# Down projection of a two-layer mixer and gated-FFN network, as seven quadrant products of Strassen's form for eight

## The chip, the core and the metric

The kernel runs on one core of one Trainium2 chip. The metric is the device time of one execution in microseconds. The kernel before took a median of 1257.42 us over 3 runs (1256.32 to 1257.91).

## The reference

One sequence of 512 tokens with 1024 channels goes through two layers. A layer is a mixer (dilated attention, a retention and a gated linear attention beside it, then `w_out`), a residual with layer norm, a gated feed-forward network with a causal convolution of width 3, and again a residual with layer norm. Only the second half matters here:

```python
def conv_glu_ffn(x, w_up, conv_w, conv_b, w_down):
    u = causal_dwconv(x @ w_up, conv_w, conv_b)
    gate, val = jnp.split(u, 2, axis=-1)
    return (jax.nn.silu(gate) * val) @ w_down
...
        ffn = conv_glu_ffn(x, w_up[l], conv_w[l], conv_b[l], w_down[l])
        x = layer_norm(DEEPNORM_ALPHA * x + ffn, ln2_g[l], ln2_b[l])
```

All arrays are float32. `w_up` is 1024 x 5632 and `w_down` is 2816 x 1024, so the gated activations have 2816 = 22 x 128 channels.

## The kernel before

**Precision.** Every large product is made of three matmuls. Each operand is split into a high part, rounded to the matmul format float32r, and a low part that holds the rest; `mm3` (L202 to L205) adds high x high, high x low and low x high in the same accumulator. The high part is a copy on ScalarE, the low part a subtraction on VectorE.

**Weights.** The host packs all weights in order of use. `weight_tile` (L180) loads one tile of up to 128 x 1024 by a DMA that SP issues into `raw` (2 buffers), casts it on ScalarE to `whi` (L189) and subtracts on VectorE to `wlo` (L190); `whi` and `wlo` have 5 buffers each. `chunk` does so for all tiles of a product.

**Up projection.** The tokens lie in columns: `xth` and `xtl` hold the high and low part of the layer's input, 128 channels by 8 blocks by 512 tokens. For each of 22 blocks of 128 activation channels, `up` (L749) makes the gate and the value rows, 2 x 8 x 3 matmuls of 512 tokens. `conv` (L738) applies the convolution, one ScalarE pass (L741) and two VectorE ones (L742, L743). `glu` (L759) applies silu, multiplies (L762) and splits the activation in a high and a low page (L766, L767). A page is a 128 x 512 tile; pools named `pg`, `yt`, `yrg` and `rope` hold 9, 14, 8 and 4 of them.

**Down projection.** It is done in two halves of 11 activation blocks, f = 0 and f = 1, each behind its own part of the up projection. `token_gemm` (L383) makes, for each half h of the 1024 output columns, four accumulators of 128 tokens by 512 columns, with the activation page as the stationary operand and the weights as the moving one. `residual` (L377) adds an accumulator to the residual rows `x0` to `x3` on VectorE (L379), and for f = 1 collects statistics (L381). In the last call, f = 1 and h = 1, the last 9 k-steps go tile by tile, so that tile t is finished 27 matmuls ahead of tile t + 1:

```python
        for t in range(NT):
            for i in range(n - tail, n):
                step(i, t)
                if t >= 2 and i == n - tail + 3:
                    to_columns()
            done(ps[t], t)
```

`done` then normalises the tile with `norm_rows` (L343): a few small VectorE instructions for the scale, and four of 512 columns (L354, L357). In layer 1 the rows go out by DMA; in layer 0 `to_columns` (L364) transposes them on TensorE and splits them into the next `xth` and `xtl`.

**Order and buffers.** A scheduler orders each engine's instructions ahead of time by its own estimate of when each is ready; every engine then takes its list strictly in order. PSUM has 8 banks: 3 `acc`, 1 `side`, 4 `sm` (named bk). The pool `x4` has 3 buffers of 128 x 2048; during the feed-forward network one holds the norm's scale and shift (`gb`), which GpSimd's queue loads.

Of the kernel before, what the change touches and what calls it, by code (L numbers as in the profile page):

```python
# [17 lines left out]
P = 128  # L18
# [22 lines left out]
def weight_chunks():  # L41

    w = {}
    every = tuple(range(KD))
    c = (("w_in", 1536, 1792), ("w_in", 3072, 3088))
    w["ret_qk"] = [(ks, c) for ks in ((0, 1, 2), (3, 4, 5), (6, 7))]
    w["gla_q"] = [(every, (("w_in", 2304, 2432),))]
    w["gla_k"] = [(every, (("w_in", 2432, 2560),))]
    for name, c in (
        ("values", (("w_in", 1792, 2048), ("w_in", 2560, 2816))),  # L50
        ("heads0", heads(0)),
        ("v", (("w_in", 1024, 1536),)),
        ("heads1", heads(1)),
        ("gates", (("w_in", 2048, 2304), ("w_in", 2816, 3072))),
    ):
        w[name] = [(ks, c) for ks in PAIRS]
    for h in range(2):
        c = (("w_out", h * 512, h * 512 + 512),)
        w[f"out{h}"] = [(ks, c) for ks in (PAIRS[2], PAIRS[3], PAIRS[0], PAIRS[1])]
    for f in range(2):  # L60
        for j in range(NFH):
            m = (f * NFH + j) * P
            c = (("w_up", m, m + P), ("w_up", D_FF + m, D_FF + m + P))
            w[f"up{f}_{j}"] = [((0, 1, 2, 3), c), ((4, 5, 6, 7), c)]
        for h in range(2):
            c = (("w_down", h * 512, h * 512 + 512),)
            k0 = f * NFH
            w[f"down{f}_{h}"] = [(tuple(range(k0 + a, min(k0 + a + 2, k0 + NFH))), c) for a in range(0, NFH, 2)]
    return w

def width(cols):
# [69 lines left out]
def hymba(ctx: ExitStack, tc: tile.TileContext, x, xt, wpk, prm, wal, lnv, cst, out):  # L141
# [57 lines left out]
    def at(priority):  # L199
        tc.cur_priority = priority  # L200

    def mm3(ps, ah, al, bh, bl, first, last):  # L202
        nc.tensor.matmul(ps, ah, bh, start=first, stop=False)  # L203
        nc.tensor.matmul(ps, ah, bl, start=False, stop=False)  # L204
        nc.tensor.matmul(ps, al, bh, start=False, stop=last)  # L205

    mmul = nc.tensor.matmul
    V = nc.vector
# [196 lines left out]
    for l in range(DEPTH):  # L405
# [338 lines left out]
            return u  # L744

        stats = [sp.tile([P, 12], F32, tag="stats", name=nm("st"), bufs=8) for _ in range(NT)]
        for f in range(2):
            rows = []
            def up(pss, kt, cols, first, last, columns_at=()):  # L749
                for gv in range(2):  # L750
                    ms = slice(gv * P, (gv + 1) * P)
                    for k in range(KD):
                        h_, l_ = kt[k]
                        if gv * KD + k in columns_at:
                            to_columns()
                        mm3(pss[gv][:, cols], h_[:, ms], l_[:, ms], xth[:, k, cols], xtl[:, k, cols],
                            first and k == 0, last and k == KD - 1)

            def glu(pss, j):  # L759
                us = [conv(pss[gv], gv * NF + f * NFH + j) for gv in range(2)]  # L760
                A.activation(out=us[0], in_=us[0], func=AF.Silu)
                V.tensor_mul(us[1], us[0], us[1])  # L762
                tag = "yrg" if j < 4 else "yt"
                h_ = page(tag, 512, F32R)
                l_ = page(tag, 512, F32R)
                A.copy(h_, us[1])  # L766
                V.tensor_sub(l_, us[1], h_.bitcast(F32))  # L767
                rows.append((h_, l_))

            j0 = 0  # L770
            if f == 0:
                early_cols, late_cols = slice(0, S // 2), slice(S // 2, S)
                kts = [chunk(l, f"up{f}_{j}") for j in range(2)]
                pss = [[acc(), acc()], [acc(), side()]]
                up(pss[0], kts[0], early_cols, True, False)
                up(pss[1], kts[1], early_cols, True, False, (2, 15))
                for j in range(2):
                    up(pss[j], kts[j], late_cols, False, True)
                    glu(pss[j], j)
                j0 = 2  # L780
            for j in range(j0, NFH):
                kt = chunk(l, f"up{f}_{j}")
                pss = [acc(), acc()]
                up(pss, kt, slice(0, S), True, True)
                glu(pss, j)
            if f == 1:
                gb = load_gb(2 * l + 1)
                if l < DEPTH - 1:
                    xth = xp.tile([P, KD, S], F32R, tag="xth", name=nm("xth"))
                    xtl = xp.tile([P, KD, S], F32R, tag="xtl", name=nm("xtl"))  # L790
            for h in range(2):
                kt = chunk(l, f"down{f}_{h}")

                def done(ps, t):
                    residual(ps, t, h, ALPHA if f == 0 else 1.0, f == 1)
                    if f == 1 and h == 1:
                        norm_rows(t, gb, l == DEPTH - 1)
                        if l < DEPTH - 1:
                            pending.append(t)

                token_gemm(rows.__getitem__, kt, 9 if f and h else 4, done)

# [36 lines left out]
```

## Time and profile before

| what | value |
|---|---|
| median of 3 runs | 1257.42 us |
| the profiled execution, its own time | 1255.33 us |
| its span on the core | 1253.6 us |
| TensorE busy (PE) | 1233.8 us, 98% |
| VectorE busy (DVE) | 786.7 us, 63% |
| ScalarE busy (ACT) | 453.1 us, 36% |
| GpSimd busy (POOL) | 15.9 us, 1% |
| mean granted TensorE clock | 0.998 |
| read from HBM | 112.93 MB, 92 GB/s over the span |

Busy is the sum of the recorded durations, as a share of the span. Matmuls are pipelined and their ends are modelled, so that a busy TensorE can hold overlapping records. A group line of the profile has the line and engine, the operation, out<-in by the program's names, the shapes and the count, then busy us, mean ns of one, and the idle time before them with what ended it. A timeline line has start and duration in us; what stands in brackets is the idle time before it. A row of stretches has the stretch, its length, then for each engine busy us and (instructions), the granted clock, the DMA share and GB/s. A line of waits has the total, the count and the longest.

### The profile page before, as it was taken

Reading aid. Unit: us, or ns where it says so; the run is one execution under the profiler, and the core shown is the slowest. Engines: PE = TensorE matmul, PEld = TensorE weight load, DVE = VectorE, ACT = ScalarE, POOL = GpSimd, SP = SyncE. Lnnn points to the kernel's source line nnn. Section 1 sums busy time; section 2 is a strip of 40 time slices with the busy share of each in tenths; the row PEclk is TensorE's granted clock in tenths of the full one; section 3 lists DMA queues with packets and bytes.
Section 4 is the critical chain, followed back from the end, with each engine's and each line's share of the span. In section 5 each row is a group of like instructions: output and inputs, shape, how many; then the busy total and the mean of one; then the engine's idle time right before and its main releaser. Section 6 shows DMA issues by size and latency. Waiting matters only on the chain.

```text
span 1253.6 us, 15361 instructions
## 1 busy us (share of the span) xinstructions
PE 1233.8 (98%) x6020; PEld 1004.1 (80%) x6020; DVE 786.7 (63%) x1519; ACT 453.1 (36%) x629; POOL 15.9 (1%) x26
## 2 busy tenths in 40 slices
PE   9999999999999999999999999999999999999997
PEld 7777777798888888888887777778988888888885
DVE  5677676687664356664767757767766633566646
ACT  4413445135442134442142134451444422444410
POOL 0010000000000000000000000000000000000000
PEclk9999999999999999999999999999999999999999
DMA  8402322224233332232142023232333322333221
GB/s 289 135 18 68 101 68 74 95 67 126 93 89 105 93 101 92 93 101 76 61 134 85 1 68 101 68 102 67 96 107 101 101 76 93 118 101 102 93 76 67
DMA packets 33399, 116.01 MB, mean 93 GB/s; under 512 B 3728, under 2 KB 4144, under 8 KB 33200
## 3 DMA queue, kind: packets, MB, share of 16 engines
q1 hardware_dynamic: 32176, 110.85, 28.0%
q0 software_dynamic: 1152, 4.19, 1.0%
q8 instruction: 47, 0.77, 0.3%
q14 instruction: 24, 0.20, 0.0%
HBM read 112.93 MB, written 2.10 MB: 92 GB/s over the span
## 4 chain that ended last, share of the span: by engine, by line
PE 90%; DMA 4%; DVE 3%; ACT 2%; issue 0%; SPq 0%; DVEq 0%; ACTq 0%
PE acc L205 25%; PE acc L203 25%; PE acc L204 25%; DMA raw<-in_wpk 4%; PE bk L277 3%; PE side L204 2%; PE side L203 2%; PE side L205 2%; DVE wlo L190 2%; ACT whi L189 2%; PE bk L636 2%; PE bk L606 1%; PE side L277 1%; PE bk L529 1%; PE bk L535 1%; PE bk L549 1%
## 5 line engine op out<-in xcount | busy, mean ns | idle before, releaser
L190 DVE TENSOR_TENSOR wlo<-raw,whi 128x1024 fp32r<-128x1024 f32 (+2 forms) x201 | 240.2, 1196 | 227.3 <-ACT whi L189 226.2
L189 ACT CAST whi<-raw 128x1024 fp32r<-128x1024 f32 (+2 forms) x201 | 206.2, 1026 | 342.6 <-PE side L205 133.8
L204 PE MATMUL acc<-xtl,whi 128*128 128x512 f32 (+1 forms) x768 | 288.7, 376 | 0.0
L205 PE MATMUL acc<-xth,wlo 128*128 128x512 f32 (+1 forms) x768 | 288.6, 376 | 0.0
L203 PE MATMUL acc<-xth,whi 128*128 128x512 f32 (+1 forms) x768 | 288.6, 377 | 0.0
L203 PEld LDWEIGHTS acc<-xth,whi 128*128 128x128 f32 x768 | 144.2, 188 | 27.5 <-issue 1.5
L204 PEld LDWEIGHTS acc<-xtl,whi 128*128 128x128 f32 x768 | 144.5, 188 | 26.5 <-DVE xtl L375 0.4
L205 PEld LDWEIGHTS acc<-xth,wlo 128*128 128x128 f32 x768 | 144.5, 188 | 26.3
L205 PE MATMUL acc<-whi,xtl 128*128 128x512 f32 (+1 forms) x384 | 147.8, 385 | 0.0
L203 PE MATMUL acc<-whi,xth 128*128 128x512 f32 (+1 forms) x384 | 147.2, 384 | 0.6 <-ACT whi L189 0.6
L204 PE MATMUL acc<-wlo,xth 128*128 128x512 f32 (+1 forms) x384 | 145.8, 380 | 0.7 <-DVE wlo L190 0.7
L203 PE MATMUL acc<-whi,yt 128*128 128x512 f32 x238 | 93.1, 391 | 0.0
L205 PE MATMUL acc<-whi,yt 128*128 128x512 f32 x238 | 92.9, 390 | 0.0
L204 PE MATMUL acc<-wlo,yt 128*128 128x512 f32 x238 | 92.6, 389 | 0.0
L205 PEld LDWEIGHTS acc<-whi,xtl 128*128 128x128 f32 x384 | 72.1, 188 | 15.6 <-issue 3.9
L203 PEld LDWEIGHTS acc<-whi,xth 128*128 128x128 f32 x384 | 72.3, 189 | 15.1 <-issue 3.2
L204 PEld LDWEIGHTS acc<-wlo,xth 128*128 128x128 f32 x384 | 72.2, 188 | 15.1 <-issue 2.2
L742 DVE SCALAR_TENSOR_TENSOR pg<-acc,prm,pg 128x511 f32<-128x511 f32 x86 | 64.2, 747 | 31.8 <-ACT pg L741 31.8
L741 ACT ACTIVATE pg<-acc,prm 128x512 f32<-128x512 f32 x86 | 66.9, 778 | 26.4 <-PE acc L205 26.4
L743 DVE SCALAR_TENSOR_TENSOR pg<-acc,prm,pg 128x510 f32<-128x510 f32 x86 | 64.4, 749 | 3.0
L379 DVE SCALAR_TENSOR_TENSOR x<-x,acc 128x512 f32<-128x512 f32 x38 | 26.1, 687 | 61.8 <-PE acc L205 61.8
L203 PE MATMUL acc<-whi,yrg 128*128 128x512 f32 x138 | 54.4, 394 | 0.0
(176 smaller groups left out, 1523.9 us busy)
## 6 DMA issues: line engine op xcount, KB each, us to landing
raw<-in_wpk SPq DMA_DIRECT2D x188, 512.0 KB, 3.6
gb<-in_lnv POOLq DMA_DIRECT2D x8, 512.0 KB, 4.6
x<-in_x SPq DMA_DIRECT2D x4, 512.0 KB, 5.9
raw<-in_wpk SPq DMA_DIRECT2D x8, 256.0 KB, 2.8
out<-x SPq DMA_DIRECT2D x8, 256.0 KB, 2.0
raw<-in_wpk SPq DMA_DIRECT2D x4, 408.0 KB, 3.5
xraw<-in_xt SPq DMA_DIRECT2D x3, 512.0 KB, 7.5
cst<-in_cst SPq DMA_DIRECT2D x1, 1222.0 KB, 8.6
```

The source lines that it names most:

```text
L189: nc.scalar.copy(hi, raw)
L190: lo_engine.tensor_sub(lo, raw, hi.bitcast(F32))
L203: nc.tensor.matmul(ps, ah, bh, start=first, stop=False)
L204: nc.tensor.matmul(ps, ah, bl, start=False, stop=False)
L205: nc.tensor.matmul(ps, al, bh, start=False, stop=last)
L277: nc.tensor.transpose(dst, src, ident)
L379: V.scalar_tensor_tensor(out=xr, in0=xr, scalar=scale, in1=ps, op0=ALU.mult, op1=ALU.add)
L529: mmul(sc, kT, qbd, start=True, stop=True)
L636: mmul(oT[hh * 64:hh * 64 + 64, j * P:], vv[:, j, c0 + hh * 64:c0 + hh * 64 + 64], pts[hh][:, o:o + n], start=j == 0, stop=js == groups[-1])
L741: A.activation(out=u, in_=ps, func=AF.Identity, scale=w(2), bias=w(3))
L742: V.scalar_tensor_tensor(out=u[:, 1:], in0=ps[:, :S - 1], scalar=w(1), in1=u[:, 1:], op0=ALU.mult, op1=ALU.add)
L743: V.scalar_tensor_tensor(out=u[:, 2:], in0=ps[:, :S - 2], scalar=w(0), in1=u[:, 2:], op0=ALU.mult, op1=ALU.add)
```

## The change

The activations H (22 blocks by 512 tokens) and `w_down` are cut in quadrants. With the tokens 256 to 511 as "late" and 0 to 255 as "early", A11 and A21 are the late and early half of blocks 0 to 10, A12 and A22 those of blocks 11 to 21. B11 and B12 are the left and right 512 columns of the first 11 blocks of `w_down`, B21 and B22 those of the others. The eight quadrant products become seven, each of 11 k-steps by 2 token tiles of 128 by 3 matmuls:

- P11 = A11 B11 and P12 = A12 B21, added into the same two banks, alpha. Their 22 steps are put between the up projection's blocks 11 to 21, two a block. Between the two, ScalarE copies P11 out (`p1`, which takes one of the 5 `wlo` buffers).
- Four products in one pass over k: beta = S2 (B22 + B12 + B11), eps = A22 (B22 + B21 + B12 + B11), delta = R1 (B12 + B11), gamma = S3 (B22 + B12). They use all 8 banks. R1 = A22 - A21 and S3 = A11 - A21 replace A21 and A11 in place, on GpSimd, during the last blocks of the up projection; S2 = S3 + A22 is made on VectorE.
- zeta = (S2 - A12) B22, the last product; its operand replaces A12, on GpSimd.

In the pass each k-step loads its four weight quadrants as one tile of 128 x 2048 (1 MB) into `x4`, of which `gb` leaves two buffers. GpSimd makes four sums in place (L870 to L873), ScalarE casts the whole tile (L875) and VectorE makes its low part (L876), into halves of a tile that takes the place of `xth` and `xtl`. The activations are no longer split in `glu`, but per use: H[k] as it is (h0, l0) and the pair S2, A22 (h1, l1). Those of P11, P12 and zeta are split into `rope` pages (L798, L799).

After the pass VectorE combines: the early rows x0 and x1 need beta, eps, delta and gamma and are normalised while zeta runs; the late rows x2 and x3 need alpha, beta, delta and zeta.

```diff
-        for f in range(2):
-            rows = []
...
-            for h in range(2):
-                kt = chunk(l, f"down{f}_{h}")
...
-                token_gemm(rows.__getitem__, kt, 9 if f and h else 4, done)
+            if j >= NFH:
+                for _ in range(2 if j < NF - 2 else 1):
+                    st, k = steps.pop(0)
+                    st(k)
+                    if st is p11 and k == NFH - 1:
+                        p1 = wp.tile([P, 1024], F32, tag="wlo", name=nm("p1"), bufs=5)
+                        for i in range(2):
+                            A.copy(p1[:, i * 512:(i + 1) * 512], alpha[i])
...
+        while steps:
+            st, k = steps.pop(0)
+            st(k)
...
+        wth = xp.tile([P, 2, 4, 512], F32R, tag="xth", name=nm("wth"))
+        wtl = xp.tile([P, 2, 4, 512], F32R, tag="xtl", name=nm("wtl"))
+        beta, eps, delta, gamma = [bank(), bank()], [acc(), acc()], [acc(), side()], [bank(), bank()]
+        for k in range(NFH):
+            o, nk, w = offsets[l, f"dall{k}"][0]
+            raw = x4("wraw")
+            nc.sync.dma_start(out=raw.rearrange("p a c -> p (a c)"),
+                              in_=wpk[o:o + P * nk * w].rearrange("(p n) -> p n", p=P))
+            G.tensor_add(raw[:, 0, :], raw[:, 0, :], raw[:, 2, :])
+            G.tensor_add(raw[:, 2, :], raw[:, 2, :], raw[:, 3, :])
+            G.tensor_add(raw[:, 3, :], raw[:, 0, :], raw[:, 3, :])
+            G.tensor_add(raw[:, 1, :], raw[:, 3, :], raw[:, 1, :])
+            th, tl = wth[:, k % 2], wtl[:, k % 2]
+            A.copy(th, raw)
+            V.tensor_sub(tl, raw, th.bitcast(F32))
+            s2 = page()
+            V.tensor_add(s2[:, :256], S3(k), A22(k))
+            h0, l0 = two_parts(H[k], "pg")
+            h1, l1 = page("pg", 512, F32R), page("pg", 512, F32R)
+            for cs, src in ((slice(0, 256), s2[:, :256]), (slice(256, 512), A22(k))):
+                A.copy(h1[:, cs], src)
+                V.tensor_sub(l1[:, cs], src, h1[:, cs].bitcast(F32))
+            G.tensor_sub(A12(k), s2[:, :256], A12(k))
+            for ps, (ah, al), q, n in ((beta, (h1, l1), 0, 3), (eps, (h1, l1), 256, 1),
+                                       (delta, (h0, l0), 0, 2), (gamma, (h0, l0), 256, 0)):
+                for i in range(2):
+                    ts = slice(q + i * P, q + (i + 1) * P)
+                    mm3(ps[i], ah[:, ts], al[:, ts], th[:, n, :], tl[:, n, :], k == 0, k == NFH - 1)
...
+        p3 = product(zeta, "d22", A12)
+        for k in range(4):
+            p3(k)
+        for i in range(2):
+            early_rows(i)
...
+        for k in range(4, NFH - 3):
+            p3(k)
+        got = [p3(k, (0,)) for k in range(NFH - 3, NFH)]
...
+        late_rows(0)
+        to_columns()
+        for k, g in zip(range(NFH - 3, NFH), got):
+            p3(k, (1,), g)
+        to_columns()
+        late_rows(1)
```

How the order of instructions changes is shown at two places of layer 0. The first is the steady part of the down projection. In before, VectorE there splits weights for h = 1 (`wlo`) and takes up accumulators (`x_82` to `x_85` are the residual rows x0 to x3, `st` their statistics):

```order
L190 TENSOR_TENSOR wlo_4721<-raw_4718,whi_4720 128x1024
L379 SCALAR_TENSOR_TENSOR x_82<-x_82,acc_4568 128x512
L381 BN_STATS st_2375<-x_82 128x6
L379 SCALAR_TENSOR_TENSOR x_83<-x_83,acc_4569 128x512
L381 BN_STATS st_2376<-x_83 128x6
```

In the change VectorE's list in the pass repeats five instructions a step. Here is one step and the next step's low part (`wraw` is the raw weight tile, `wtl` its low part, `pg` are h1, l1, h0, l0 and s2, `yt` are activations):

```order
L773 TENSOR_TENSOR pg_4796<-yt_3158,pg_4795 128x512
L883 TENSOR_TENSOR pg_4800<-pg_4793,pg_4799 128x256
L883 TENSOR_TENSOR pg_4800<-yt_4176,pg_4799 128x256
L878 TENSOR_TENSOR pg_4838<-yt_3231,yt_4275 128x256
L876 TENSOR_TENSOR wtl_4416<-wraw_4785,wth_4415 128x2048
```

Each of these reads two tiles, and none of them an accumulator (`acc`, `bk` or `side`), where L379 reads one tile and one accumulator. GpSimd's list in before has nothing at this place but the load of `gb`, and goes on with the next layer:

```order
L717 DMA gb_4527<-in_lnv 128x1024 x2
L557 TENSOR_TENSOR pg_5441<-pg_5034,cst 128x128
L533 TENSOR_TENSOR pg_5447<-yrg_5206,cst 128x512
L557 TENSOR_TENSOR pg_5489<-pg_5034,cst 128x128
L533 TENSOR_TENSOR pg_5496<-yrg_5206,cst 128x512
```

In the change its list at the same steps is this:

```order
L870 TENSOR_TENSOR wraw_4785<-wraw_4785 128x512
L871 TENSOR_TENSOR wraw_4785<-wraw_4785 128x512
L872 TENSOR_TENSOR wraw_4785<-wraw_4785 128x512
L873 TENSOR_TENSOR wraw_4785<-wraw_4785 128x512
L884 TENSOR_TENSOR yt_4275<-pg_4838,yt_4275 128x256
```

So four sums of 512 columns and one difference of 256 stand on GpSimd for every step of the pass, and VectorE's low part of a tile (L876) follows its sums by way of ScalarE's cast.

The second place is the end of the layer. In before, TensorE ends with the last matmuls of tile x3 (`side`) and has the transposes of x1 (`cst` is the identity) in their midst:

```order
L205 MATMUL side_4751<-whi_4726,yt_4144 128x512
L277 MATMUL bk_4940<-cst,x_83 128x128 x4
L277 MATMUL bk_4947<-cst,x_83 128x128 x4
L203 MATMUL side_4751<-whi_4732,yt_4219 128x512
L204 MATMUL side_4751<-wlo_4733,yt_4219 128x512
```

In the change TensorE is at the fifth step, k = 4, of the last product (bk_4924 and bk_4925 are zeta; rope_5034 and rope_5035 the high and low rows of k = 4 and 5; x_82 is x0):

```order
L209 MATMUL bk_4925<-whi_4954,rope_4959 128x512
L207 MATMUL bk_4924<-whi_5030,rope_5034 128x512
L208 MATMUL bk_4924<-wlo_5031,rope_5034 128x512
L207 MATMUL bk_4925<-whi_5030,rope_5034 128x512
L208 MATMUL bk_4925<-wlo_5031,rope_5034 128x512
L281 MATMUL bk_5126<-cst,x_82 128x128 x4
L281 MATMUL bk_5133<-cst,x_82 128x128 x4
L209 MATMUL bk_4924<-whi_5030,rope_5035 128x512
```

VectorE reaches the last instructions of x0 (L361) and the low rows rope_5035 (L799) here:

```order
L907 BN_STATS st_2376<-x_83 128x6
L361 SCALAR_TENSOR_TENSOR x_82<-x_82,s_ln_4987,gb_4376 128x512 x2
L350 BN_AGGR s_ln_5009<-st_2376 128x2
L918 TENSOR_TENSOR x_85<-x_85,p_3882 128x512
L352 TENSOR_SCALAR s_ln_5011<-s_ln_5009 128x1
L358 SCALAR_TENSOR_TENSOR x_83<-x_83,s_ln_5009,gb_4376 128x512
L308 TENSOR_SCALAR s_ln_5013<-s_ln_5011 128x1
L358 SCALAR_TENSOR_TENSOR x_83<-x_83,s_ln_5009,gb_4376 128x512
L310 TENSOR_TENSOR s_ln_5014<-s_ln_5013 128x1
L799 TENSOR_TENSOR rope_5035<-yt_3767,rope_5034 128x256
```

From the first use of beta (L895) to rope_5035 VectorE's list has 26 instructions of 512 columns. Four steps of the last product and four matmuls of the fifth stand before the transposes of x0 on TensorE, and behind those the next matmuls wait for the rows of k = 4.

More of the change, by code (lines that the diff above doesn't have):

```diff
@@ L746, in hymba @@
         stats = [sp.tile([P, 12], F32, tag="stats", name=nm("st"), bufs=8) for _ in range(NT)]
-        for f in range(2):
-            rows = []
[L749 to L790, printed above, removed]
-            for h in range(2):
-                kt = chunk(l, f"down{f}_{h}")
[L794 to L799, printed above, removed]
-                token_gemm(rows.__getitem__, kt, 9 if f and h else 4, done)
@@ new lines, in hymba, with up, glu @@
+        H = []
+        def up(pss, kt, cols, first, last, columns_at=()):
+            for gv in range(2):
+                ms = slice(gv * P, (gv + 1) * P)
+                for k in range(KD):
+                    h_, l_ = kt[k]
+                    if gv * KD + k in columns_at:
+                        to_columns()
+                    mm3(pss[gv][:, cols], h_[:, ms], l_[:, ms], xth[:, k, cols], xtl[:, k, cols],
+                        first and k == 0, last and k == KD - 1)
+        def glu(pss, j):
+            us = [conv(pss[gv], gv * NF + j) for gv in range(2)]
+            A.activation(out=us[0], in_=us[0], func=AF.Silu)
+            h_ = page("yrg" if j < 8 else "yt")
+            V.tensor_mul(h_, us[0], us[1])
+            H.append(h_)
@@ new lines, in hymba @@
+        early_cols, late_cols = early, late
+        kts = [chunk(l, f"up0_{j}") for j in range(2)]
+        pss = [[acc(), acc()], [acc(), side()]]
+        up(pss[0], kts[0], early_cols, True, False)
+        up(pss[1], kts[1], early_cols, True, False, (2, 15))
+        for j in range(2):
+            up(pss[j], kts[j], late_cols, False, True)
+            glu(pss[j], j)
+        alpha = None
+        for j in range(2, NF):
+            kt = chunk(l, f"up{j // NFH}_{j % NFH}")
+            pss = [acc(), acc()]
+            up(pss, kt, slice(0, S), True, True)
+            glu(pss, j)
+            if j == NFH:
+                alpha = [bank(), bank()]
+                p11 = product(alpha, "d11", A11)
+                p12 = product(alpha, "d21", A12, False)
+                steps = [(p11, k) for k in range(NFH)] + [(p12, k) for k in range(NFH)]
+            if j >= NFH:
[6 more added lines that the diff above has]
+                            A.copy(p1[:, i * 512:(i + 1) * 512], alpha[i])
+                if j >= NFH + 6:
+                    for k in ((0, 1, 2) if j == NFH + 6 else (j - NFH - 4,) if j < NF - 1 else ()):
+                        G.tensor_sub(A11(k), A11(k), A21(k))
+                        G.tensor_sub(A21(k), A22(k), A21(k))
```

90 lines of the change are left out of this document (83 added, 7 removed).

## The prediction

> **What bounds the kernel now.** I read the page first: the busy shares and the chain that ended last.
>
> ```profile
> PE 1233.8 (98%) x6020; PEld 1004.1 (80%) x6020; DVE 786.7 (63%) x1519; ACT 453.1 (36%) x629; POOL 15.9 (1%) x26
> ...
> PE 90%; DMA 4%; DVE 3%; ACT 2%; issue 0%; SPq 0%; DVEq 0%; ACTq 0%
> ```
>
> TensorE is the bound nearly everywhere, and GpSimd is idle. What one matmul is worth comes next, since a busy time can overlap its neighbour. The groups by shape give the durations that I need; this one is the largest of the down projection:
>
> ```profile
> L203 PE MATMUL acc<-whi,yt 128*128 128x512 f32 x238 | 93.1, 391 | 0.0
> ```
>
> The timeline of TensorE in the last down projection shows starts 0.22 to 0.23 us apart, though each is listed with 0.39 us:
>
> ```profile
> 1232.05 0.39 PE L203 MATMUL acc<-whi,yrg 128*128 128x512 f32 x1
> 1232.27 0.39 PE L204 MATMUL acc<-wlo,yrg 128*128 128x512 f32 x1
> ```
>
> The timeline of VectorE at the same place gives it exactly. L379 takes a finished token tile; between two tiles lie 9 k-steps of 3 matmuls:
>
> ```profile
> 1232.25 0.69 DVE L379 SCALAR_TENSOR_TENSOR x<-x,acc 128x512 f32<-128x512 f32 x1 [0.40 <-PE acc L205]
> ...
> 1238.37 0.69 DVE L379 SCALAR_TENSOR_TENSOR x<-x,acc 128x512 f32<-128x512 f32 x1 [0.40 <-PE acc L205]
> ...
> 1244.49 0.69 DVE L379 SCALAR_TENSOR_TENSOR x<-x,side 128x512 f32<-128x512 f32 x1 [0.40 <-PE side L205]
> 1245.21 0.69 DVE L381 BATCH_NORM_STATS2 st<-x 128x6 f32<-128x512 f32 x1
> ...
> 1246.25 0.74 DVE L354 SCALAR_TENSOR_TENSOR x<-x,s_ln,gb 128x512 f32<-128x512 f32 x1
> ...
> 1246.97 0.74 DVE L354 SCALAR_TENSOR_TENSOR x<-x,s_ln,gb 128x512 f32<-128x512 f32 x1
> ...
> 1248.79 1.41 DVE L357 SCALAR_TENSOR_TENSOR x<-x,s_ln,gb 128x512 f32<-128x512 f32 x2
> ```
>
> 6.12 us for 27 matmuls is 0.227 us each. The stretch of the up projection agrees (150 us for 663 recorded matmuls, 0.226), with VectorE at half load and GpSimd at nothing:
>
> ```profile
> 305.00:455.00 150.00, 150.00 (x663) 124.02 (x662) 73.92 (x87) 50.98 (x62) 0.00 (x0) 1.00 0.31 95
> ```
>
> In the down projection VectorE waits for TensorE; 32 waits of this kind fill 61.8 us:
>
> ```profile
> DVE x L379 <- PE acc L205: 61.8, 32, 4.8
> ```
>
> So a removed 512-column matmul is worth 0.227 us, as long as nobody else becomes late.
>
> **What is removed.** Down took 4 token tiles x 2 column halves x 22 k x 3 = 528 matmuls a layer. Seven products of 11 k x 2 tiles x 3 are 462. That is 66 a layer, 132 in all: 132 x 0.227 = **-29.9 us**. At the listed 0.39 us it would be 51, which the spacing excludes.
>
> **What the pass adds.** The pass does four products in 11 steps of 24 matmuls, so TensorE needs 24 x 0.227 = 5.44 us a step. Each step now also needs work on the other engines. Durations by shape, from the groups:
>
> ```profile
> L190 DVE TENSOR_TENSOR wlo<-raw,whi 128x1024 fp32r<-128x1024 f32 x188 | 230.0, 1224 | 222.6 <-ACT whi L189 221.6
> L189 ACT CAST whi<-raw 128x1024 fp32r<-128x1024 f32 x188 | 197.0, 1049 | 328.5 <-PE side L205 122.3 <-DMA raw<-in_wpk 73.4 <-PE acc L205 62.2
> ...
> L533 POOL TENSOR_TENSOR pg<-yrg,cst 128x512 f32<-128x512 f32 x8 | 8.3, 1041 | 75.6 <-DVE yrg L471 51.8 <-PE bk L545 23.8
> ...
> L297 DVE TENSOR_TENSOR rope<-acc,cst 128x256 f32<-128x256 f32 x16 | 6.7, 417 | 0.0
> ...
> L190 DVE TENSOR_TENSOR wlo<-raw,whi 128x512 fp32r<-128x512 f32 x8 | 5.5, 692 | 2.8 <-ACT whi L189 2.7
> ...
> L189 ACT CAST whi<-raw 128x512 fp32r<-128x512 f32 x8 | 5.0, 624 | 5.4 <-PE side L205 4.4 <-DMA raw<-in_wpk 1.0
> ...
> L557 POOL TENSOR_TENSOR pg<-pg,cst 128x128 f32<-128x128 f32 x6 | 2.8, 474 | 490.0 <-DVE s_ln L308 423.9 <-PE bk L529 47.8 <-DMA cst<-in_cst 18.3
> ```
>
> - GpSimd: four 512-column sums, 4 x 1.04 = 4.16 us, and one 256-column difference, 0.6 us (between the 0.40 us of an undisturbed 128-column one, shown below, and 1.04). Together 4.8.
> - VectorE: the low part of 2,048 weight columns, 1.22 + 1,024 x 1.04 ns (the slope between 0.69 and 1.22) = 2.29; row parts 0.69 + 2 x 0.42; one sum 0.42. Together 4.24.
> - ScalarE: 2,048 columns, 1.05 + 0.85 = 1.90; 0.62 and 2 x 0.41 for rows. Together 3.3.
>
> Each alone is below 5.44. Two couplings are not.
>
> *The ring of raw buffers.* Of the three x4 buffers one holds the norm's vectors, so two hold raw weights. The load of step k+2 waits on SP until VectorE's low part of step k is done; then load, sums, cast and low part follow one another. The load is 1 MB; smaller ones took this long to land:
>
> ```profile
> raw<-in_wpk SPq DMA_DIRECT2D x188, 512.0 KB, 3.6
> ...
> raw<-in_wpk SPq DMA_DIRECT2D x8, 256.0 KB, 2.8
> ```
>
> 0.8 us per 256 KB more gives 5.2 (an estimate). The ring is 5.2 + 4.16 + 1.90 + 2.29 = 13.6, with handovers 14.0, for two steps: 7.0 us a step against 5.44.
>
> *GpSimd and VectorE shut each other out.* The timeline of VectorE, then that of GpSimd, at two places:
>
> ```profile
> 41.95 0.68 DVE L316 SCALAR_TENSOR_TENSOR yt<-s_rg,acc 128x512 f32<-128x512 f32 x1
> 42.54 1.16 DVE L469 TENSOR_TENSOR yrg<-yrg,yrg 128x512 f32<-128x512 f32 x1
> ...
> 63.83 0.48 DVE L509 SCALAR_TENSOR_TENSOR yt<-yt,yrg,yt 128x256 f32<-128x256 f32 x1
> ...
> 67.23 0.42 DVE L562 TENSOR_TENSOR pg<-bk,cst 128x256 f32<-128x256 f32 x1 [0.63 <-PE bk L560]
> ```
>
> ```profile
> 42.11 1.04 POOL L533 TENSOR_TENSOR pg<-yrg,cst 128x512 f32<-128x512 f32 x1 [22.95 <-DVE yrg L471]
> 63.94 0.62 POOL L557 TENSOR_TENSOR pg<-pg,cst 128x128 f32<-128x128 f32 x1 [20.79 <-PE bk L529]
> 66.79 1.04 POOL L533 TENSOR_TENSOR pg<-yrg,cst 128x512 f32<-128x512 f32 x1 [2.22 <-PE bk L545]
> 71.27 0.40 POOL L557 TENSOR_TENSOR pg<-pg,cst 128x128 f32<-128x128 f32 x1 [3.44 <-PE bk L529]
> ```
>
> L469 reads two SBUF tiles. It met GpSimd's multiply and took 1.16 instead of 0.69, ending 0.55 after GpSimd ended at 43.15: it had waited. At 63.94 GpSimd met L509, which was ahead, and took 0.62 instead of 0.40. L316 and L562, which read one operand from PSUM, ran beside GpSimd at their usual length. So the instruction that comes second waits for the first, if VectorE reads two SBUF tiles. All five VectorE instructions of a pass step do (2.29 + 0.69 + 0.84 + 0.42), and all five of GpSimd. Then a step costs at most 4.8 + 4.24 = 9.0; at least 7.6, if each of ten instructions hides the 0.14 of start-up that L469 hid (0.69 - 0.55). I take 8.2, about the middle: some instructions will hide their start-up, while the first steps also carry row and weight splits for the last product.
>
> The Trainium skill, "SBUF — State Buffer", section "Who interferes with whom", states this as an exclusive lock: a VectorE instruction with two SBUF inputs and a GpSimd one that reads SBUF do not share, the later blocks fully. By that rule in full, 9.0 us a step, the sum below would be about 1316; the trace's two collisions agree with it.
>
> The weights of steps 0 and 1 are summed during the up projection, so nine steps pay 8.2 - 5.44 = 2.76: 25 us a layer.
>
> *The start.* The high and low parts overwrite xth and xtl, so they wait for the last up matmul. Then ScalarE does a conv pass and the cast (0.78 + 1.90), VectorE the 2.29; row casts sit behind the second cast. Twelve leftover matmuls cover 2.7 of that; I count 3 us. Adding P11 into P12's banks makes TensorE wait for two copies of alpha, about 1. **Pass and start: 2 layers x (25 + 4) = +58 us**; between 2 x (19.4 + 4) = 47, at 7.6 a step, and 2 x (32 + 4) = 72, at 9.0.
>
> **The last product.** It has 66 matmuls, 15 us. Behind the pass VectorE has 23 instructions of 512 columns before x0 is normalised and 26 before the rows of k = 4, at about 0.66 us from start to start, with a microsecond of small ones: 16 and 18.5 us from the end of beta, which lies 15 matmuls, 3.4 us, before the end of the pass. So x0 comes 12.6 and the rows, with their own 0.42, 15.5 after that end. TensorE has done its 28 matmuls after 6.3, waits for x0, spends some 0.9 on eight transposes and waits again until 15.5: 8.3 idle. In layer 1 there is no transpose, and it is idle for 9. **+17.** In before this normalisation lay under matmuls of the next tiles. I bound the 17 by 8, if VectorE reaches the rows half as late, and 22, if each of its 26 instructions takes its full 0.75.
>
> **The end.** Tiles 2 and 3 now finish 9 matmuls (2 us) apart, not 27, and their norms interleave: 7.6 us for the last instead of the 5.7 from 1244.49 to 1250.20. **+2.** In the up projection a step with leftover products has 60 matmuls, 13.6 us. By the row of that stretch VectorE had 74 / 150 x 10.9 = 5.4 us of work in 48 of them; it loses the row split (0.69) and gains a third weight tile (1.22) and two row parts (0.84): 6.8, which the matmuls hide. The row differences on GpSimd and the two early sets of sums hide there too. Without that cover they would cost their excess over 13.6.
>
> **Sum.** The profiled run took 1255.33 with a span of 1253.6; the median of the three runs is 1257.42, 2.1 more. 1255.3 - 29.9 + 58 + 17 + 2 = 1302.4 in its terms; I put the median 2 higher, at **1304**.
>
> **Rivals.**
> 1. *The ring alone paces* (the exclusion, seen only in single collisions, hides in the ring's own idle time): 9 x (7.0 - 5.44) = 14 a layer; 1255.3 - 29.9 + 2 x (14 + 4) + 19 = 1280, median 1282. For it: the ring has 7.1 us of load and cast in which nobody reads twice. Against: the other buffer's ring fills that time with 9.0 of its own.
> 2. *TensorE stays the bound, so the change is faster.* It decides if two steps of the ring take under 10.9 us, that is if load and four sums come in under 6.7 instead of 9.4. Then 1255.3 - 29.9 + 8 + 19 = 1252, median 1254, and some 9 less if the last product's wait is at its lower bound. For it: every engine alone is under 5.44. Against: the eight 512-column GpSimd instructions of before average 1.04, so four sums leave 2.5 us for a load whose half took 3.6.
> 3. *Gains and losses cancel*: a loss of 30 in all, with steps barely over 5.44; 1257.
> 4. *The clock falls too.* The granted clock by stretch:
>
> ```profile
> 5.00:10.00 5.00, 3.78 (x17) 2.90 (x16) 3.08 (x4) 3.03 (x5) 0.00 (x0) 1.00 0.99 370
> 1245.00:1253.60 8.60, 0.00 (x0) 0.00 (x0) 4.89 (x15) 0.00 (x0) 0.00 (x0) 0.74 0.24 91
> ```
>
> It stayed 1.00 with a quarter of 5 us idle and fell only where no matmul ran. If the gaps of about 3 us in each step halved it, 24 matmuls would take 10.9 us, 2.7 more than a step's 8.2. Over all 22 steps that is 59, over half of them 30: 1334 to 1363.
>
> **Chances.** Exclusion as forecast (1293 to 1318 by its bounds, and 6 more for the last product's) 0.66, ring alone 0.15, worse, the clock among it, 0.09, faster 0.06, cancelled 0.04. A measurement here tells 0.2% (2.5 us) from no change. The range reaches from 1268, the ring alone with the last product at its lower bound (1273) and a load landing a little sooner, to 1330, where the clock's case begins: it leaves out 0.06 + 0.04 + 0.09 = 0.19. Slower 0.90, same 0.04, faster 0.06.
>
> **What would show it.** Right: matmuls of the pass still 0.227 apart, in groups with gaps; steps of about 8.2 us; GpSimd's sums and VectorE's low parts longer than 1.04 and 2.29 where they meet; TensorE waiting for wtl and, behind the pass, for x0 and rope. Wrong: steps of 5.4 us with no wait on wtl or on wth, sums of 1.04 beside running low parts, or a last product without gaps.

## The result, and the profile after

| | before | after |
|---|---|---|
| median of 4 runs each | 1256.87 us (1255.35 to 1257.91) | 1333.45 us (1333.29 to 1333.65) |
| ratio, 95% interval | | 1.061 (1.0592 to 1.0629) |
| span of the profiled execution | 1253.6 us | 1331.9 us |
| mean granted clock | 0.998 | 0.97 |

The change makes the kernel 76.6 us slower. The forecast was 1304, with a range to 1330: slower as forecast, but by 76.6 instead of 46.6, and just outside the range.

The page of after, its busy times and the shares of the chain by engine:

```profile
PE 1247.2 (94%) x5888; PEld 996.9 (75%) x5888; DVE 930.9 (70%) x1647; ACT 506.7 (38%) x731; POOL 229.9 (17%) x180
...
PE 76%; DVE 12%; POOL 4%; DMA 3%; ACT 2%; issue 2%; POOLq 0%; SPq 0%; DVEq 0%; ACTq 0%
```

The 132 matmuls are gone (6020 to 5888), yet TensorE is listed as busy for longer: a matmul is longer where the clock is lower (0.63 us at a granted clock of 0.50 behind the wait in the last product, 0.39 at 1.00). VectorE and GpSimd now stand in the chain. The waits of TensorE say where (in all, times, longest, in us):

```profile
PE bk L208 <- DVE wtl L876: 19.6, 11, 2.4
PE bk L209 <- DVE pg L883: 12.9, 8, 2.4
PE bk L209 <- DVE rope L799: 8.9, 3, 7.3
PE bk L281 <- DVE x L361: 4.1, 1, 4.1
```

The first two are the pass (low parts of weights and of rows), the last two the last product. No wait of the pass is over 2.4 us; they are many and short.

One step of the steady pass, first GpSimd's timeline, then VectorE's (start, duration):

```profile
591.10 1.30 POOL L870 TENSOR_TENSOR wraw<-wraw 128x512 f32<-128x512 f32 x1
592.47 3.22 POOL L871 TENSOR_TENSOR wraw<-wraw 128x512 f32<-128x512 f32 x1
595.77 1.62 POOL L872 TENSOR_TENSOR wraw<-wraw 128x512 f32<-128x512 f32 x1
597.46 1.35 POOL L873 TENSOR_TENSOR wraw<-wraw 128x512 f32<-128x512 f32 x1
599.58 0.73 POOL L884 TENSOR_TENSOR yt<-pg,yt 128x256 f32<-128x256 f32 x1 [0.76 <-DVE pg L878]
600.26 1.27 POOL L870 TENSOR_TENSOR wraw<-wraw 128x512 f32<-128x512 f32 x1
```

```profile
591.61 2.93 DVE L876 TENSOR_TENSOR wtl<-wraw,wth 128x2048 fp32r<-128x2048 f32 x1 [1.35 <-ACT wth L875]
594.47 1.77 DVE L773 TENSOR_TENSOR pg<-yrg,pg 128x512 fp32r<-128x512 f32 x1
596.16 1.51 DVE L883 TENSOR_TENSOR pg<-pg,pg 128x256 fp32r<-128x256 f32 x1
597.60 1.50 DVE L883 TENSOR_TENSOR pg<-yt,pg 128x256 fp32r<-128x256 f32 x1
```

The ends interlock. L871 starts at 592.47, while L876 runs to 594.54, and ends at 595.69: 1.15 us behind it, nearly one sum's length. L773 starts at 594.47 and ends at 596.24, 0.55 behind L871. So they take turns all through the step, which is 600.26 - 591.10 = 9.16 us long; VectorE's 0.69 has become 1.77, its 0.42 has become 1.50. A sum that meets nobody takes 1.27 to 1.30.

The starts of ScalarE's casts of steps 2 to 10, in layer 0 (count, shortest, median and longest in ns, first and last start):

```profile
L875 ACT CAST wth<-wraw x9: 1898/1907/1912, 547.4 to 626.2; 128x2048 fp32r<-128x2048 f32 x9
```

(626.2 - 547.4) / 8 = 9.85 us a step; in layer 1 it is 9.92. TensorE needs 5.44.

The last product, by stretches of 5 us (TensorE's, VectorE's and the other engines' busy time, the granted clock, DMA):

```profile
640.00:645.00 5.00, 2.05 (x10) 1.36 (x8) 5.00 (x17) 0.00 (x0) 0.00 (x0) 0.99 0.00 0
645.00:650.00 5.00, 2.60 (x10) 2.11 (x11) 5.00 (x15) 1.78 (x4) 0.00 (x0) 0.50 0.00 0
650.00:655.00 5.00, 5.00 (x13) 3.92 (x12) 3.54 (x10) 0.71 (x2) 0.00 (x0) 0.50 0.27 84
655.00:660.00 5.00, 5.00 (x23) 4.05 (x22) 3.78 (x8) 1.95 (x3) 0.00 (x0) 0.98 0.28 84
```

VectorE is full for 10 us while TensorE waits, as forecast. From 645 to 655 the clock is 0.50, and 13 matmuls fill 5 us where 23 do at 0.98: that was not in the sum.

Where the 78.3 us between the two spans lie, by starts of matmuls in both traces (us):

| stage | before | after | difference | forecast |
|---|---|---|---|---|
| layer 0, first up matmul to the next layer's first | 364.5 | 399.0 | +34.5 | |
| layer 1, first up matmul to the last matmul | 362.5 | 397.5 | +35.0 | |
| both: removed, pass, last product | | | +69.5 | -29.9 + 58 + 17 = +45 |
| layer 1, its first matmul to the first up matmul | 255.2 | 260.7 | +5.6 | 0 |
| behind the last matmul | 9.5 | 12.0 | +2.5 | +2 |

The other 0.8 us lie ahead of layer 0's first up matmul.

### The profile page after: what moved, and what is told of

The parts are those of the page before. It is cut to its first block, busy times and chain, and to the rows that moved or that the text cites. A ratio compares the mean times of both kernels' runs of the same rounds, so it can differ in the third digit from the quotient of the medians.

```text
span 1331.9 us, 15643 instructions
## 1 busy us (share of the span) xinstructions
PE 1247.2 (94%) x5888; PEld 996.9 (75%) x5888; DVE 930.9 (70%) x1647; ACT 506.7 (38%) x731; POOL 229.9 (17%) x180
## 4 chain that ended last, share of the span: by engine, by line
PE 76%; DVE 12%; POOL 4%; DMA 3%; ACT 2%; issue 2%; POOLq 0%; SPq 0%; DVEq 0%; ACTq 0%
PE acc L209 19%; PE acc L208 19%; PE acc L207 19%; PE bk L281 3%; DMA raw<-in_wpk 3%; PE bk L209 2%; DVE wlo L193 2%; PE bk L208 2%; PE bk L207 2%; DVE wtl L876 2%; PE bk L640 2%; DVE pg L883 1%; PE bk L610 1%; ACT whi L192 1%; POOL wraw L871 1%
## 5 line engine op out<-in xcount | busy, mean ns | idle before, releaser
L193 DVE TENSOR_TENSOR wlo<-raw,whi 128x1024 fp32r<-128x1024 f32 (+3 forms) x189 | 237.3, 1257 | 133.0 <-ACT whi L192 115.9
L192 ACT CAST whi<-raw 128x1024 fp32r<-128x1024 f32 (+3 forms) x189 | 194.1, 1028 | 212.4 <-DMA raw<-in_wpk 89.5
L875 ACT CAST wth<-wraw 128x2048 fp32r<-128x2048 f32 x22 | 41.9, 1906 | 85.6 <-POOL wraw L873 79.9
L876 DVE TENSOR_TENSOR wtl<-wraw,wth 128x2048 fp32r<-128x2048 f32 x22 | 58.8, 2671 | 20.0 <-ACT wth L875 20.0
L209 PE MATMUL bk<-whi,rope 128*128 128x512 f32 x132 | 55.1, 420 | 8.9 <-DVE rope L799 8.9
L208 PE MATMUL bk<-wtl,pg 128*128 128x512 f32 x88 | 38.5, 437 | 19.6 <-DVE wtl L876 19.6
L870 POOL TENSOR_TENSOR wraw<-wraw 128x512 f32<-128x512 f32 x22 | 32.6, 1480 | 139.2 <-DMA wraw<-in_wpk 138.6
```

The lines of the kernel that those rows point to most:

```text
L192: nc.scalar.copy(hi, raw)
L193: lo_engine.tensor_sub(lo, raw, hi.bitcast(F32))
L208: nc.tensor.matmul(ps, ah, bl, start=False, stop=False, skip_group_check=more)
L209: nc.tensor.matmul(ps, al, bh, start=False, stop=last, skip_group_check=more)
L870: G.tensor_add(raw[:, 0, :], raw[:, 0, :], raw[:, 2, :])
L875: A.copy(th, raw)
```

## Experiments

Theory A is that of the prediction: GpSimd's and VectorE's two-input instructions shut each other out, and their sum paces the pass. The rivals are the ring of two raw buffers, and the clock. Unless a number of runs is given, a time is that of one execution; the kernel before took 1256.2 to 1262.2 beside them.

**No sums.**

```diff
-            G.tensor_add(raw[:, 0, :], raw[:, 0, :], raw[:, 2, :])
-            G.tensor_add(raw[:, 2, :], raw[:, 2, :], raw[:, 3, :])
-            G.tensor_add(raw[:, 3, :], raw[:, 0, :], raw[:, 3, :])
-            G.tensor_add(raw[:, 1, :], raw[:, 3, :], raw[:, 1, :])
```

> The four sums of weight quadrants on GpSimd are left out, so the products use the raw quadrants (this leaves out the sums of the Strassen form, and the result is another one). Theory A, GpSimd and VectorE shut each other out and their sum paces a pass step: what is left is 0.73 + 4.24 = 5.0 us, under TensorE's 5.44, and the ring is load 4.9 + cast 1.9 + low part 2.3 = 9.1 for two steps, so the pass runs at TensorE's 5.4 to 5.8 us a step and the kernel takes about 1333 - 2 x 36 = 1261 (1253 to 1272). Theory B, it is VectorE and ScalarE that cannot prepare a step in time, with or without sums: steps stay above 7 us and the time above 1290. Theory C, the granted clock that falls is the larger part: the clock stays near 1.00 in the pass here if it falls through waiting, and the gain is the same as in A; it falls as in the changed kernel if it falls through anything else, and the time stays above 1300.

Measured 1261.9. The casts of steps 2 to 10:

```profile
L871 ACT CAST wth<-wraw x9: 1912/1914/1921, 548.6 to 593.4; 128x2048 fp32r<-128x2048 f32 x9
```

5.60 us a step, near TensorE's 5.44: the sums, and what they do to their neighbours, are nearly all that holds the steps up. This run alone can't tell the exclusion from the ring, since the sums are part of both. And without them the kernel is still no faster than before.

**The ring: three raw buffers.** The norm's vectors are loaded behind the pass:

```diff
-        gb = load_gb(2 * l + 1)
         while steps:
...
+        gb = load_gb(2 * l + 1)
         u2 = [p1[:, i * 512:(i + 1) * 512] for i in range(2)]
```

> The norm's vectors are loaded behind the pass, so that the raw weights have three buffers instead of two; everything is computed. Theory A, the sum of the GpSimd and VectorE instructions paces, at 9.1 to 10: a third buffer changes nothing in the steady steps, 1325 to 1335. Theory B, the ring of two buffers paces (load 4.9, sums, cast, low part, in turn): with three buffers a ring takes a third of its time a step, so steps fall by a third to about 6.2 us and the kernel to about 1270.

Measured 1310.7, between the two. Steps fall only to 9.0 on average (5.4 to 12.8 singly), so something other than the ring paces too; the next runs show what:

```profile
L874 ACT CAST wth<-wraw x9: 1898/1908/1917, 546.8 to 618.9; 128x2048 fp32r<-128x2048 f32 x9
```

**The exclusion: GpSimd writes only.** The four sums become four times

```diff
+            G.memset(raw[:, 0:3, :], 0.5)
```

> In place of each of the four sums GpSimd fills three of the four quadrants of the raw tile with a constant (this leaves out the sums, and most of the weights of the four products): GpSimd stays busy and the chain load, GpSimd, cast, low part stays, but GpSimd reads no SBUF operand. Theory A, GpSimd's sums and VectorE's instructions with two SBUF inputs exclude each other: fills beside them exclude nobody, the low part is back at 2.29 us, and if a fill lasts about 1.3 us the step is paced by the ring at (4.9 + 5.2 + 1.9 + 2.3) / 2 = 7.2 us, about 1285. Theory B, it is only GpSimd's occupation in the ring: as in the changed kernel, steps of 9 us and 1333. Theory C, any GpSimd instruction blocks VectorE, read or write: the low part stays at 2.7 on average and steps at 9, 1333. Where a fill lasts another time than 1.3 us, both sides are worked out again with its duration from the trace.

Measured 1315.0. The groups, and the casts:

```profile
L876 DVE TENSOR_TENSOR wtl<-wraw,wth 128x2048 fp32r<-128x2048 f32 x22 | 50.7, 2304 | 47.5 <-ACT wth L875 47.5
...
L871 POOL MEMSET wraw<- 128x1536 f32 x22 | 30.4, 1381 | 0.6
```

```profile
L875 ACT CAST wth<-wraw x9: 1897/1899/1912, 550.8 to 618.2; 128x2048 fp32r<-128x2048 f32 x9
```

A fill lasts 1.38, as long as a sum, in the same place; yet the low part is back at 2.30 from 2.67, also where fills run beside it for 2.2 of its 2.29 us, and L773 is back at 0.69 from 1.52. So it is GpSimd's reading that shuts VectorE out, not its being busy. Theory A's time was still 30 us too low: a step takes 8.4, not 7.2. The trace shows why. GpSimd's list has the fills of two steps interleaved, so that one step's four last 7.5 to 7.9 us from first to last; load, fills, cast and low part are 4.9 + 7.5 + 1.9 + 2.3 = 16.6 for two steps, and 16.9 are measured. The ring alone is slower than theory A and its rival had it.

**Both.** Three raw buffers and fills in one kernel.

> Both of the last two edits in one: three raw buffers, and four fills of 1.38 us in place of the four sums on GpSimd (this leaves out the sums, and most of the weights of the four products). Theory A, two limits of nearly the same size lie on each other, GpSimd and VectorE shutting each other out (9.0 to 9.3 us a step with three buffers) and the ring of two raw buffers (8.4 with fills that exclude nobody): with both gone GpSimd's own 4 x 1.38 + 0.74 = 6.3 is the largest, steps of 6.3 to 6.8 us, and the kernel takes 1333 - 18 x 3.2 = 1275 (1268 to 1283). Theory B, the two edits did the same thing by two ways: no more than the better of them alone, 1305 to 1312.

Measured 1276.8, 56.6 less than the changed kernel, where the two edits alone brought 22.8 and 18.4; steps are 6.8. Two limits lay on each other, at 9.0 and 8.4 us: neither edit alone can show what either is worth.

**Sums on VectorE.** `G.tensor_add` becomes `V.tensor_add` in the four lines.

> The four sums run on VectorE, not on GpSimd; everything is computed. Theory A, mutual exclusion: the sum of both engines falls only by what a VectorE add is shorter than a GpSimd one, 4 x (1.29 - 0.69) = 2.4 us, and adds at most the start-up that is hidden between neighbours, so a step takes 4 x 0.6 + 4.24 + 0.73 = 7.0 to 7.7 us instead of 9.1 to 9.9, and the kernel 1285 to 1300. Theory B, only the ring of two buffers paces: 4.9 + 2.6 + 1.9 + 2.3 = 11.7 for two steps, 5.9 a step, about 1268. Theory C, VectorE must not be given more, since it is the busy one: 4 x 0.69 + 4.24 = 7.0 us of its own with waits behind it, 9 or more a step, 1330 or slower.

Measured 1303.1, at 7.6 to 7.8 us a step: a little over theory A's range, and neither B nor C. What was not expected stands in GpSimd's timeline. It kept one small difference a step, which now lies in VectorE's stream:

```profile
568.56 8.14 POOL L884 TENSOR_TENSOR yt<-pg,yt 128x256 f32<-128x256 f32 x1 [3.50 <-DVE pg L878]
...
592.36 1.05 POOL L884 TENSOR_TENSOR yt<-pg,yt 128x256 f32<-128x256 f32 x1 [7.26 <-DVE pg L878]
```

Where nothing is in its way it takes 0.73; the longest of the 22 took 10.68. VectorE's instructions here have their usual 0.68 and 2.28: the one that waits is GpSimd, and VectorE then stands 0.63 us for its result.

**GpSimd out of the pass.** All on VectorE, and three raw buffers:

```diff
+            V.tensor_add(raw[:, 0, :], raw[:, 0, :], raw[:, 2, :])
+            V.tensor_add(raw[:, 2, :], raw[:, 2, :], raw[:, 3, :])
+            V.tensor_add(raw[:, 3, :], raw[:, 0, :], raw[:, 3, :])
+            V.tensor_add(raw[:, 1, :], raw[:, 3, :], raw[:, 1, :])
...
+            V.tensor_sub(A12(k), s2[:, :256], A12(k))
```

> GpSimd is taken out of the pass: the four sums and the difference of rows run on VectorE, and the raw weights have three buffers; everything is computed. Theory A: what is left is VectorE's own work, by starts that follow each other 4 x 0.66 + 2.25 + 0.66 + 4 x 0.33 = 6.9 us a step, and no exclusion; steps of 6.9 to 7.3 and 1333 - 18 x 2.8 = 1283 (1275 to 1292). Theory B, VectorE with sums in its queue makes TensorE wait in turn, as with the sums on VectorE alone: steps of 7.6 and 1300. On neither does it beat the kernel before.

Measured 1281.6. A stretch of the pass, and the first and last of the ten VectorE instructions of a step with the start of the next:

```profile
575.00:590.00 15.00, 13.87 (x58) 10.27 (x57) 15.00 (x26) 7.60 (x9) 0.00 (x0) 1.00 0.51 194
```

```profile
582.70 0.68 DVE L869 TENSOR_TENSOR wraw<-wraw 128x512 f32<-128x512 f32 x1
...
588.92 0.41 DVE L883 TENSOR_TENSOR yt<-pg,yt 128x256 f32<-128x256 f32 x1
589.25 0.68 DVE L869 TENSOR_TENSOR wraw<-wraw 128x512 f32<-128x512 f32 x1
```

VectorE is busy for 15.00 of 15 us, and the step is 589.25 - 582.70 = 6.55 us (6.88 on average over steps 2 to 10): VectorE's own work, and the clock stays at 1.00 beside it.

**One sum back on the idle engine.** This one tells most sharply; the edit is against the kernel just above:

```diff
-            V.tensor_add(raw[:, 0, :], raw[:, 0, :], raw[:, 2, :])
+            G.tensor_add(raw[:, 0, :], raw[:, 0, :], raw[:, 2, :])
```

> As the kernel with everything on VectorE and three raw buffers, but one of the four sums goes back to GpSimd; everything is computed. This takes 0.66 us a step off the engine that is busy without a pause and gives it to an idle one. Theory A, the two engines exclude each other, so their sum counts: 6.55 - 0.66 + 1.29 = 7.2 us a step, and 18 x 0.63 = 11 us slower, about 1293 (1287 to 1300). Theory B, they work side by side, and GpSimd was slow in the changed kernel only for its own load and the ring: 5.9 us a step, about 1270 (1266 to 1275).

Measured 1293.2, and steps of 7.3 on average, where the kernel above has 6.88:

```profile
L874 ACT CAST wth<-wraw x9: 1899/1916/1919, 548.3 to 606.7; 128x2048 fp32r<-128x2048 f32 x9
```

Taking work off the full engine and giving it to an empty one costs 11.6 us between two single executions; 8.2 of them lie in the two passes, 78.3 and 79.2 us long instead of 74.9 and 74.4. Two engines that exclude each other have one budget, and there a GpSimd sum is dearer (1.29) than a VectorE one (0.68).

**The clock in the pass.**

```diff
+            for _ in range(8 if k > 1 else 0):
+                mmul(beta[0][:64, :256], C("zeros"), A22(0), start=False, stop=False, skip_group_check=True)
```

> TensorE gets eight matmuls with a zero operand, whose result adds nothing, ahead of the 24 of each step of the pass from k = 2 on, so that it has 24 x 0.227 + 8 x 0.43 = 8.9 us of work in a step of 9.1 to 9.9. Theory A, the step is paced by GpSimd and VectorE, and the lower clock (0.77 in parts of the pass) only stretches matmuls into time that was idle: the time stays within 1328 to 1340. Theory B, the lower clock is itself what makes steps 9.9 instead of 8.2, since TensorE then frees the weight buffers late: the clock stays at 1.00 and the steps go to about 8.9, the kernel to 1315 or lower.

Measured 1341.1. A stretch of the pass, in after and in this run:

```profile
575.00:590.00 15.00, 12.00 (x39) 9.26 (x40) 13.65 (x13) 4.70 (x8) 12.59 (x9) 0.77 0.38 141
```

```profile
575.00:590.00 15.00, 15.00 (x66) 10.19 (x65) 11.68 (x9) 4.04 (x6) 14.08 (x10) 1.00 0.37 141
```

and the casts:

```profile
L875 ACT CAST wth<-wraw x9: 1899/1913/1915, 547.4 to 627.1; 128x2048 fp32r<-128x2048 f32 x9
```

The clock is 1.00 where the changed kernel had 0.77 in the same 15 us, and a step still takes 9.96 us. This alone does not refute theory B: TensorE is full here, 15.00 of 15 us, since the eight fills take 3.67 us and its step 9.26, and ScalarE waits for it (10.5 us in six waits from 575 to 626). The trace of after settles it. From 590 to 626, its steady steps, the casts wait 19.8 us for GpSimd's sums, and all waits of other engines for TensorE come to 1.1 us. So the lower clock only stretches matmuls into idle time; theory B falls. From the last cast to the end of the first pass there are 13.6 us here instead of 9.1.

**The clock in the last product.** The same fills, 9 in layer 0 and 16 in layer 1, behind `p3(3)`, into `zeta[0]` with `A12(NFH - 1)`.

> TensorE gets matmuls with a zero operand, whose result adds nothing, 9 in layer 0 and 16 in layer 1, at the place where it waits 4.1 and 7.3 us in the last product; everything else is as in the changed kernel. Theory A, the granted clock falls after these gaps and the next 13 matmuls run at 0.43 us instead of 0.23, the transposes at half speed too: with the gap filled they run at full speed, 3 to 4 us a layer less, about 1326 (1322 to 1330). Theory B, the time in the last product is VectorE's alone, since TensorE waits for it whatever its clock: 1332 to 1335. If a filling matmul lasts longer than 0.43 us, it fills more than the gap and the time rises by the excess.

Measured 1325.9, 7.5 less. Three of the stretches that were shown for after, now in this run:

```profile
640.00:645.00 5.00, 5.00 (x23) 2.96 (x22) 5.00 (x16) 0.00 (x0) 0.00 (x0) 1.00 0.00 0
645.00:650.00 5.00, 3.12 (x17) 2.13 (x16) 5.00 (x18) 1.78 (x4) 0.00 (x0) 1.00 0.00 0
650.00:655.00 5.00, 5.00 (x23) 4.13 (x23) 4.97 (x11) 2.00 (x4) 0.00 (x0) 1.00 0.27 89
```

The clock holds, and from 650 there are 23 matmuls in 5 us instead of 13. The last products are 2.8 and 2.3 us shorter: so much the lower clock cost in them. That is rival 4 in part: here, but not in the pass.

**The order of the last product.** All its steps go ahead of the normalisation:

```diff
-        for k in range(4):
+        for k in range(NFH):
             p3(k)
         for i in range(2):
             early_rows(i)
...
-        for k in range(4, NFH - 3):
-            p3(k)
-        got = [p3(k, (0,)) for k in range(NFH - 3, NFH)]
...
-        for k, g in zip(range(NFH - 3, NFH), got):
-            p3(k, (1,), g)
```

> The changed kernel with another order in the last product: all 11 steps, with their splits of rows and weights, stand ahead of the normalisation of the first two token tiles, so that TensorE isn't held up in the middle of its 66 matmuls; everything is computed. Theory A, the wait in the last product is one of order, since VectorE normalises first and splits rows late: 66 matmuls take 15 us in one piece, and what VectorE still has to do behind them lies partly under the next layer's first matmuls; 4 to 5 us less in layer 0 and 3 to 4 in layer 1, about 1325 (1321 to 1330). Theory B, it is VectorE's amount of work behind the pass, in whatever order: the wait moves to the next layer's start and to the end, 1331 to 1337.

Measured 1332.5, which looks like theory B. By stages it isn't: this execution was 5.6 us late before the first pass began, in code that is the same, and 8.4 us ahead behind the two passes. So more executions were timed.

> The changed kernel with the last product in one piece ahead of the normalisation, the same edit as in the single look, now timed in rounds. Theory A, a wait of order: in the single look the way from the end of the first pass to the end of the kernel was 4.1 us shorter in layer 0 and 4.3 in layer 1, and the 5.6 us that came up before the first pass, in code that is the same, were chance; the median is then 1323 to 1328. Theory B, VectorE's amount of work: 1331 to 1335, as the single look's whole time says.

The median of 4 runs is 1325.2 (1323.7 to 1326.6), 1.0542 of the kernel before (1.0523 to 1.0561): theory A. The 66 matmuls take 15.0 us in one piece, where after has 25.3 and 24.8. Of these 20.2 us 10.9 come back where VectorE's work now lies: the next layer's start, up to its first up matmul, is 5.4 us longer (266.2 instead of 260.7) and the end 5.5 (17.5 instead of 12.0). So about half of the wait was one of order and half one of amount. TensorE's waits for rope are gone, and one for x0 is left, longer than before but later:

```profile
PE bk L281 <- DVE x L361: 6.9, 1, 6.9
```

**Combinations.** Everything on VectorE with three raw buffers, once with the fills and once with the other order.

> Everything on VectorE, three raw buffers, and the filling matmuls with a zero operand in the last product; everything is computed. The terms lie behind one another, so they add: 1281.6 - 7.6 = 1274 (1272 to 1276). If the clock of the last product is already held up by the shorter gaps of this pass, the fill brings nothing: 1281.

> Everything on VectorE, three raw buffers, and the last product in one piece ahead of the normalisation; everything is computed. By theory A of the order (a wait of order) 1281.6 - 8 = 1273 (1270 to 1278); by theory B (VectorE's amount of work) 1280 to 1285. Neither reaches the 1257 of the kernel before, since 11 x 1.1 us of the pass and its start stay in each layer.

Measured 1277.2 and 1279.6, against 1274 and 1273 expected. The kernel before took 1262.2 beside these two, and 1256.2 beside the kernel with everything on VectorE that they start from, so that part of the miss may be chance. The stages say more. The fills shorten the two last products by 2.8 and 2.4 us, as in the changed kernel. The order shortens them by 21.4 us, but 16.2 come back, 9.0 at the next layer's start and 7.2 at the end, where it was 10.9 in the changed kernel; why more, was not tested. Neither is near the kernel before. These are the best versions found that compute everything.

**What seven products are worth.** The sums are left out, and the last product is in one piece.

> The changed kernel without the four sums (the products use the raw quadrants, so the sums of the Strassen form are left out) and with the last product in one piece ahead of the normalisation. It asks what seven products are worth if the sums cost nothing. If the two terms, the pass and the order of the last product, are all that was lost: the pass runs at 5.4 to 5.6 us a step, and 1261 less 8 gives 1253 (1249 to 1257), a little under the kernel before. If the 29.9 us of removed matmuls are really there but 20 go to the last product and the pass's start whatever the order, it is 1258 to 1262, no faster than before.

Median of 10 runs 1256.5, ratio 0.9997 (0.9986 to 1.0009): no difference from the kernel before, and at the upper edge of what the first theory had (1249 to 1257). Even with free sums and the better order the 29.9 us of removed matmuls are given back. In its profile, which is of the slowest of the ten (1263.6), the intervals between the first casts of each layer are 10.6, 8.2 and 7.5 us instead of 5.4, some 10 us a layer: the pass starts slowly. By the stages of the table above, the way from the first up matmul to the next layer, and in layer 1 to the last matmul, is 6.8 and 6.3 us shorter than before, but the next layer's start is 11.8 longer and the end 7.3.

## Why the prediction was right and wrong

**Removed matmuls: right.** 132 fewer, and where the clock is full they stand 0.227 us apart as before.

**What paces the pass: right; its size: wrong.** This is the step that failed: "four 512-column sums, 4 x 1.04 = 4.16 us", and with it "I take 8.2". The 1.04 came from a row of 128x512 sums, but of a multiplication of 128 columns, repeated for four heads, with a mask that is repeated along the columns. After still shows 1.04 for that one. A sum of two full tiles takes 1.27 to 1.30 where nothing meets it, the 256-column difference 0.73 where I put 0.6. GpSimd's part is 4 x 1.29 + 0.73 = 5.9 us, not 4.8, and with VectorE's 4.24 the bounds are 8.7 and 10.1 instead of 7.6 and 9.0. Measured are 9.15 in the steady steps and 9.85 and 9.92 on average over steps 2 to 10. Eight intervals at 9.9 instead of 8.2 are 13.5 us a layer, 27 in all. The steady 9.15 accounts for 15 of these, and GpSimd's price, 1.1 us a step too low, is enough for that. The other 12 are in the earlier steps: VectorE's list there also has splits for the last product (L193, L799), and GpSimd waits 3.6 us for a load once, at 562.79. I had named the splits, but without a price. The stages of pass and last product together missed by 24: 27 by the steps, 3 by the last product, and some 6 the other way, by a start that was shorter than I had counted.

The Trainium skill, "SBUF — State Buffer", section "Who interferes with whom", has the mechanism: a VectorE instruction with two SBUF inputs contends with a GpSimd instruction that reads SBUF, and not with one that only writes. The runs agree with both halves: 2.67 us for the low part beside sums, 2.30 beside fills. Its rule in full, the plain sum of both engines, would have been 10.1 here with the right durations; 9.15 was measured. That fits hidden start-up: L773 ends 0.55 behind L871 instead of 0.69.

**Rival 1, the ring: half right.** It doesn't pace alone, but it isn't hidden either. Without exclusion it sets 8.4 us a step (not the 7.0 that I gave it, for GpSimd's list mixes the fills of two steps), and without it steps are still 9.0. I had taken them as alternatives; removing one brings 18 or 23 us, removing both 57.

**The last product: right in size, partly by luck.** Forecast were 8.3 and 9 us of idle time; the two products are 10.3 and 9.8 us longer than 15.0. But TensorE's waits in them are 4.1 and 1.2 us in layer 0 and 7.3 in layer 1, less than forecast, since VectorE had x0 and the rows ready some 2 us sooner. The rest in layer 0 is the eight transposes, 2.0 us, and 13 matmuls at 0.43 us instead of 0.23, which the sum didn't have. VectorE's queue is what TensorE waits for, as said, but about half of it was a matter of order: with the splits first the kernel is 8 us faster. The fills took 5.0 us off the two products. That and the gain by order are not a sum: with the splits first the 66 matmuls stand 0.227 apart without any fill.

**Rival 4, the clock: right in one place.** I had priced it for the pass, where hardly anything waits for TensorE.

**The next layer's start: not seen.** +5.6 us, with no term in the sum. Its cause stays open. With the fills of the last product it is 2.0 us shorter, but other runs in which its code and the last product are as in after have 257.9 to 263.8 us against 260.7, so one run doesn't show what it hangs on.

**The end: right.** +2.5 against +2.

## What to carry to other kernels

A step that is shared out between VectorE and GpSimd has one budget, not two, as soon as VectorE's instructions have two SBUF inputs and GpSimd's read SBUF: the sum of the two is the bound (10.1 us here, 9.15 measured). Take each price from a row with the same operation and operands, and ask whether the dearer engine should have any of it. Where two limits are close, take both away in one run before calling either harmless. And count what products bring with them, not only what they save: here 29.9 us of matmuls were worth nothing even with free sums.

## What was not expected of the hardware

- GpSimd can be kept out for long: a difference of 0.73 us took 8.14, and once 10.68, beside a VectorE stream of two-input instructions, while in the changed kernel the two took turns one by one.
- The granted clock falls on waits that are short by themselves. In the pass, where no wait of TensorE is over 2.4 us, it is 0.77 over the 15 us from 575: it falls to 0.50 towards the end of a wait of 2.4 us, at 577, and is back at 1.00 from 584. So it is at 553, in a wait of 2.2, but not in another of 2.2 from 592 to 595. In the wait of 4.1 us it falls at 645 and stays at 0.50 for 10 us.
- A GpSimd instruction of 128 x 512 can cost 1.04 us or 1.29: the first is a multiplication that repeats 128 columns for four heads against a mask repeated along the columns, the second a sum of two full tiles. Whether the operation or the operands make the difference, no run shows.
